# Attention of a two-layer hybrid DiT with the keys on the partitions: row maxima from a first pass, no transposes of the probabilities, row sums by additions

## The chip, the cores and the metric

One core of a Trainium2 chip runs the whole program. The time is the device time of one execution in microseconds (us). A core has five engines with a queue each that they work off in order: TensorE (PE, with its weight loads as PEld), VectorE (DVE), ScalarE (ACT), GpSimd (POOL) and SyncE (SP), which here only issues DMAs.

## The reference

Two layers over 256 context and 1024 latent tokens of width 1024. Each layer normalises and modulates its input, projects it once, gives the parts to three branches (gated DeltaNet, GDN; latent attention, MLA; gated linear attention, GLA), gates each and projects the sum of widths back. The change lies in the attention of the MLA branch: 8 heads, queries and keys of 64 + 32 (the 32 are rotated, and shared by all heads on the key side), values of 64; context queries read context keys, latent queries read all 1280.

```python
def attend(q, k, v):
    s = jnp.einsum('bqhd,bkhd->bhqk', q, k).astype(jnp.float32) * MLA_SCALE
    p = jax.nn.softmax(s, axis=-1).astype(v.dtype)
    return jnp.einsum('bhqk,bkhd->bqhd', p, v)
# out = attend(...) * silu(z); layer 1 needs no context output
```

Everything is f32, and results have to agree with f32.

## The kernel before

The tokens are ten tiles of 128 (i = 0, 1 context, 2 to 9 latent), the heads four pairs m with hh = 0 and 1. A layer runs the input projection, prepares GDN, projects q, k and v up (`up`) into arrays in memory (qn_d, qpe_d, kn_d, kpe_d, v_d), then runs `attend`, then the output projection (`proj_start`, `proj`). Beside `up` and `attend` runs a background generator: the GDN scan of 20 steps (tiles kS, Tr, F), the preparation of GLA, its 7 levels, and the GLA scan of 10 steps (`gla_scan`, L926 to L992: kdt transposes the keys, ktl is their copy, gO the output, oL its sum, gF the state's addition, Sl the state; head_norm writes the result to y_d). All of its matmul groups use one PSUM buffer (tag "l", one buffer). `run` takes one background step after each yield of `attend` (L1481); whatever is left comes after. The framework's scheduler then sorts each engine's instructions by its own estimate of the times, and the engines run the order that it fixes.

Scores need more than one pass of the fast f32 format (fp32r), so q and k are split in a rounded part (hi: kTh, qTh, made by ACT) and the remainder (lo: kTl, qTl, made by POOL). `mm3` (L253) adds three products:

```python
mm(out, lh, rh, start=first, stop=False)
mm(out, lh, rl, start=False, stop=False)
mm(out, ll, rh, start=False, stop=last)
```

`attend` goes over units: a pair m, a 128-query tile i and a head hh (a context unit takes both tiles at once): 72 in layer 0, 64 in layer 1. The queries of a unit are stationary (128x128), and the 1280 keys move, so scores have queries on the partitions: sa holds 1024 keys (two buffers of two banks), sb 256. `first` and `second` issue them; DVE reduces the maxima (L1206, L1225, L1226), ACT makes the exponentials with the maximum as bias and their sums as a by-product (L1228, L1227). `transposed` turns the probabilities on PE, 128x128 at a time into ptr (L1243), and ACT or DVE copies them out (PT, L1247). After four units `output` multiplies: 20 matmuls O (L1255) with 64 columns of vv stationary and 256 queries of PT moving, head 0 into partitions 0 to 63 and head 1 into 64 to 127; the sums reach the same layout through a diagonal matrix dg times ones (L1266, L1267). ztl (the gate) and the division end it. `load_k` fetches the keys of a pair through one stage buffer kTs (L1150, L1151), `load_q` the queries, both some units ahead.

Of the kernel before, what the change touches and what calls it, by code (L numbers as in the profile page):

```python
# [18 lines left out]
NT = 10  # L19
T = 1280  # L20
# [8 lines left out]
KB = 4  # L29
QB = 4  # L30
QSB = 2
PTB = 2
YMB = 1
PB = 3
ATB = 3
KVB = 3
LA = 3
# [6 lines left out]
class Net:  # L44
# [969 lines left out]
    def up(self, l):  # L1014
# [79 lines left out]
        for a, b in GROUPS:  # L1094
            ps = self.g("kpt", "u")
            w = 128 * (b - a)
            for i in range(a, b):
                nc.tensor.transpose(ps[0:32, 128 * (i - a):128 * (i - a) + 128], ko[:, i, :], self.ident)
            t = uo()
            A.copy(t[0:32, :w], ps[0:32, :w])  # L1100
            P.memset(t[32:64, :w], 0.0)
            nc.sync.dma_start(self.kpe_d[l][:, 128 * a:128 * b], t[0:64, :w])
# [31 lines left out]
    def attend(self, l, fill=None):  # L1134
        nc, sp = self.nc, self.ap
# [3 lines left out]
        lt0 = CT if last else 0  # L1139
        kTs, vv = {}, {}  # L1140

        def load_k(m):
            kTs[m] = []
            vv[m] = self.ab.tile([128, T], F32, name="vv", tag="vv", bufs=2)
            nc.sync.dma_start(vv[m].rearrange("p (i c) -> p i c", c=128),
                              self.v_d[l][:, :, 128 * m:128 * m + 128].rearrange("i p c -> p i c"))
            for hh in range(2):
                st = self.ab.tile([128, T], F32, name="kTs", tag="kTs", bufs=1)
                hi, lo = (self.ab.tile([128, T], F32R, name=nm, tag="kT", bufs=KB) for nm in ("kTh", "kTl"))
                nc.sync.dma_start(st[0:64], self.kn_d[l][m, 64 * hh:64 * hh + 64])  # L1150
                nc.sync.dma_start(st[64:128], self.kpe_d[l])  # L1151
                A.copy(hi, st)  # L1152
                P.tensor_tensor(lo, st, hi.bitcast(F32), ALU.subtract)
                kTs[m].append((hi, lo))

        qTs = {}

        def load_q(m, i0):
            t0 = 128 * i0
            st = sp.tile([128, 2, 256], F32, name="qTs", tag="qTs", bufs=QSB)  # L1160
            hi, lo = (sp.tile([128, 2, 256], F32R, name=nm, tag="qT", bufs=QB) for nm in ("qTh", "qTl"))
            nc.sync.dma_start(st[0:64], self.qn_d[l][m, :, t0:t0 + 256].rearrange("(h p) t -> p h t", h=2))
            for r in (64, 96):
                nc.sync.dma_start(st[r:r + 32], self.qpe_d[l][2 * m:2 * m + 2, :, t0:t0 + 256].rearrange("h p t -> p h t"))
            A.copy(hi, st)
            P.tensor_tensor(lo, st, hi.bitcast(F32), ALU.subtract)
            zt = sp.tile([128, 256], F32, name="ztl", tag="ztl", bufs=2)
            nc.sync.dma_start(zt, self.zt_d[l][m, :, t0:t0 + 256])
            qTs[m, i0] = (hi, lo, zt)

        groups = [(m, i) for m in range(4) for i in range(lt0, NT, 2)]
        units = [(m, i + j, hh) for m, i in groups for hh in range(2) for j in range(1 if i < CT else 2)]
        sb, mxs, sas, ps, PT, rds = {}, {}, {}, {}, {}, {}

        def scores(u, dst, c0, cn, j=0):
            m, i, hh = units[u]
            q, k = [t[:, hh] for t in qTs[m, i - i % 2][0:2]], kTs[m][hh]
            J = slice(128 * (i % 2 + j), 128 * (i % 2 + j) + 128)
            self.mm3(dst, q[0][:, J], q[1][:, J], k[0][:, c0:c0 + cn], k[1][:, c0:c0 + cn], True, True)

        def prepare(u):

            for v in (u, min(u + LA, len(units) - 1)):
                m, i, hh = units[v]
                if m not in kTs:
                    load_k(m)
                if (m, i - i % 2) not in qTs:
                    load_q(m, i - i % 2)

        def first(u, c0):  # L1190

            m, i, hh = units[u]
            if i < CT:
                if c0 == 0:
                    sas[u] = sa = self.ps.tile([128, 1024], F32, name="sa", tag="sa", bufs=2)[:, 0:512]
                    for j in range(2):
                        scores(u, sa[:, 256 * j:256 * j + 256], 0, 256, j)
                    mxs[u] = mx = sp.tile([128, 2], F32, name="mx", tag="mx", bufs=4)
                    V.tensor_reduce(mx, sa.rearrange("p (j k) -> p j k", j=2), AX.X, ALU.max, negate=True)
                return  # L1200
            if c0 == 0:
                sas[u] = self.ps.tile([128, 1024], F32, name="sa", tag="sa", bufs=2)
            scores(u, sas[u][:, c0:c0 + 512], c0, 512)
            if c0 == 512:
                mxs[u] = mx = sp.tile([128, 2], F32, name="mx", tag="mx", bufs=4)
                V.tensor_reduce(mx[:, 0:1], sas[u], AX.X, ALU.max, negate=True)  # L1206

        def second(u):

            m, i, hh = units[u]  # L1210
            mx, ta = mxs.pop(u), sas.pop(u)
            if hh == 0 and i % 2 == 0:
                rds[m, i] = sp.tile([128, 2, 2, 2], F32, name="rd", tag="rd", bufs=3)
            r = rds[m, i - i % 2][:, hh, i % 2, :]
            ps[u] = p = self.ab.tile([128, T], F32, name="P", tag="P", bufs=PB)
            if i < CT:
                for j in range(2):
                    J = slice(256 * j, 256 * j + 256)
                    A.activation(p[:, J], ta[:, J], AF.Exp, bias=mx[:, j:j + 1], accum_out=r[:, j:j + 1])
                return  # L1220
            if u // 2 not in sb:
                sb[u // 2] = self.ps.tile([128, 512], F32, name="sb", tag="sb", bufs=1)
            tb = sb[u // 2][:, 256 * (u % 2):256 * (u % 2) + 256]
            scores(u, tb, 1024, 256)
            V.tensor_reduce(mx[:, 1:2], tb, AX.X, ALU.max, negate=True)  # L1225
            V.tensor_tensor(mx[:, 0:1], mx[:, 0:1], mx[:, 1:2], ALU.min)  # L1226
            A.activation(p[:, 1024:T], tb, AF.Exp, bias=mx[:, 0:1], accum_out=r[:, 1:2])  # L1227
            A.activation(p[:, 0:1024], ta, AF.Exp, bias=mx[:, 0:1], accum_out=r[:, 0:1])  # L1228

        def transposed(u, ka):  # L1230
            m, i, hh = units[u]
            nk = NT if i >= CT else 4
            if ka >= nk:
                return
            if ka == 0 and i % 2 == 0:
                PT[hh] = self.ab.tile([128, NT, 256], F32, name="PT", tag="PT", bufs=PTB)
            p, kb = ps[u], min(ka + 4, nk)
            if kb == nk:
                ps.pop(u)
# [38 lines left out]
        for u in range(n + 1):  # L1278
            if u + 1 < n:
                prepare(u + 1)  # L1280
# [303 lines left out]
```

## Time and profile before

| | us |
|---|---|
| median of 3 runs (lowest to highest) | 2279.92 (2273.16 to 2285.7) |
| profiled execution: its time / span | 2280.18 / 2278.4 |
| PE busy | 2043.3 (90%) |
| DVE, ACT, POOL busy | 1291.6, 941.1, 743.7 |
| attention of layer 0 (632 to 1075): PE, DVE, ACT, POOL busy | 408.73, 312.73, 241.78, 168.78 of 443 |
| attention of layer 1 (1755 to 2171): PE, DVE, ACT, POOL busy | 382.50, 290.18, 220.17, 157.69 of 416 |

A row of the timeline gives the start, the busy time, the engine, the line, the operation, the written tile and the read ones, shapes and count of a group; in brackets stand the idle time ahead of it on that engine and what ended it. "x4" is four records, and an f32 matmul has two records, a matmul of hi and lo parts one. Ends on PE are modelled: the distance from start to start says what a matmul costs, and the busy time has a tail in it. PEclk is the clock that was granted, as a share of full speed.

### The profile page before, as it was taken

The numbers are of one execution on the slowest core, as the hardware profiler recorded it, in microseconds if no ns is written. First come the engines' busy times: TensorE is split into PE (matmuls) and PEld (weight loads), VectorE is DVE, ScalarE is ACT, GpSimd is POOL, SyncE is SP. The second block draws the span as 40 slices with busy tenths as digits, with TensorE's granted clock in tenths as the row PEclk, the third lists the DMA queues.
The fourth block names the chain that finished last, engine by engine and source line by source line (L and its number), as shares of the span: only waits on it lengthen the run. The fifth ranks groups of instructions, "written<-read, shape, count | busy, mean of one in ns | idle before, by whom it ended". The sixth has DMA issues, their size and how long they took to land.

```text
span 2278.4 us, 44490 instructions
## 1 busy us (share of the span) xinstructions
PE 2043.3 (90%) x17820; PEld 1709.8 (75%) x17820; DVE 1291.6 (57%) x2187; ACT 941.1 (41%) x1926; POOL 743.7 (33%) x936
## 2 busy tenths in 40 slices
PE   5998997999989988898897998976987999899998
PEld 3987896886767766676897987875876776667688
DVE  3446685323447689656425356795233677975634
ACT  3246311533235466555204356212542445564531
POOL 1233265122234543214103322381123264421410
PEclk8999998899989999999898999998998999899999
DMA  7111343258742231113424212424266242101352
GB/s 296 47 62 61 105 119 113 84 200 284 220 109 76 76 111 36 40 48 121 161 93 171 65 36 81 136 69 115 90 197 168 58 115 96 54 24 50 100 155 103
DMA packets 207551, 247.34 MB, mean 109 GB/s; under 512 B 60976, under 2 KB 164464, under 8 KB 203760
## 3 DMA queue, kind: packets, MB, share of 16 engines
q1 hardware_dynamic: 207344, 244.49, 34.1%
q8 instruction: 140, 2.29, 0.4%
q14 instruction: 67, 0.55, 0.1%
HBM read 168.14 MB, written 76.28 MB: 107 GB/s over the span
## 4 chain that ended last, share of the span: by engine, by line
PE 46%; DVE 13%; ACT 5%; DMA 5%; issue 3%; POOL 2%; SPq 1%; DVEq 0%; POOLq 0%; ACTq 0%
PE O L1255 6%; PE ptr L1243 4%; PE po L257 3%; PE po L255 3%; PE po L256 3%; PE sa L255 3%; PE sa L256 2%; PE sa L257 2%; PE ptk L255 1%; PE ptk L256 1%; PE ptk L257 1%; DVE XT L634 1%; DVE X L636 1%; PE kS L730 1%; DVE acc L345 1%
## 5 line engine op out<-in xcount | busy, mean ns | idle before, releaser
L255 PE MATMUL ptk<-whi,hhi 128*128 128x256 f32 (+1 forms) x912 | 263.6, 290 | 6.1 <-DVE ev L297 2.2
L257 PE MATMUL ptk<-whi,hlo 128*128 128x256 f32 (+1 forms) x912 | 261.9, 288 | 1.8 <-POOL hlo L238 1.7
L256 PE MATMUL ptk<-wlo,hhi 128*128 128x256 f32 (+1 forms) x912 | 261.7, 287 | 0.4 <-DVE wlo L250 0.4
L1243 PE MATMUL ptr<-c_id,P 128*128 128x128 f32 x1312 | 203.6, 283 | 27.8 <-ACT PT L1247 18.8
L1243 PEld LDWEIGHTS ptr<-c_id,P 128*128 128x128 f32 x1312 | 151.2, 143 | 78.1 <-ACT PT L1247 29.9
L1247 ACT COPY PT<-ptr 128x512 f32<-128x512 f32 (+1 forms) x256 | 122.3, 480 | 211.1 <-PE ptr L1243 209.7
L256 PE MATMUL pin<-hlo,whi 128*128 128x512 f32 (+1 forms) x544 | 201.6, 371 | 1.6 <-issue 1.6
L255 PE MATMUL pin<-hhi,whi 128*128 128x512 f32 (+1 forms) x544 | 202.5, 372 | 0.0
L257 PE MATMUL pin<-hhi,wlo 128*128 128x512 f32 (+1 forms) x544 | 201.8, 372 | 0.0
L255 PEld LDWEIGHTS ptk<-whi,hhi 128*128 128x128 f32 x912 | 179.4, 197 | 10.8 <-issue 4.3
L1206 DVE TENSOR_REDUCE mx<-sa 128x1 f32<-128x1024 f32 x128 | 156.2, 1220 | 53.6 <-PE sa L257 53.0
L257 PEld LDWEIGHTS ptk<-whi,hlo 128*128 128x128 f32 x912 | 178.8, 197 | 5.3 <-POOL hlo L238 3.0
L256 PEld LDWEIGHTS ptk<-wlo,hhi 128*128 128x128 f32 x912 | 179.4, 197 | 3.1 <-issue 2.0
L1255 PE MATMUL O<-PT,vv 128*64 128x256 f32 x1312 | 169.6, 388 | 1.7 <-ACT PT L1247 0.9
L255 PE MATMUL po<-wohi,yh 128*128 128x256 f32 x576 | 164.4, 286 | 4.4 <-DVE yl L1353 2.1
L256 PE MATMUL po<-wolo,yh 128*128 128x256 f32 x576 | 164.0, 285 | 0.0
L257 PE MATMUL po<-wohi,yl 128*128 128x256 f32 x576 | 162.6, 285 | 0.0
L1228 ACT ACTIVATE P<-sa,mx 128x1024 f32<-128x1024 f32 x128 | 142.2, 1111 | 0.0
L1255 PEld LDWEIGHTS O<-PT,vv 128*64 128x64 f32 x1312 | 97.2, 138 | 59.0 <-issue 11.9
L255 PE MATMUL sa<-kTh,qTh 128*128 128x512 f32 (+1 forms) x272 | 118.3, 436 | 21.1 <-ACT kTh L1152 15.2
L250 POOL TENSOR_TENSOR wlo<-wst,whi 128x1024 fp32r<-128x1024 f32 x32 | 84.1, 2639 | 127.5 <-ACT whi L249 126.4
L256 PEld LDWEIGHTS pin<-hlo,whi 128*128 128x128 f32 x544 | 105.6, 194 | 19.7 <-issue 4.4
(341 smaller groups left out, 5030.6 us busy)
## 6 DMA issues: line engine op xcount, KB each, us to landing
wada<-in_w_ada_dram SPq DMA_DIRECT2D x24, 1024.0 KB
wst<-in_w_in_dram SPq DMA_DIRECT2D x48, 512.0 KB
kv<-ktv_d SPq DMA_DIRECT2D x80, 128.0 KB
wost<-in_w_out_dram SPq DMA_DIRECT2D x16, 512.0 KB
xt<-in_x_all_dram SPq DMA_DIRECT2D x10, 512.0 KB
at_d<-D SPq DMA_DIRECT2D x4, 1280.0 KB
kn_d<-uo SPq DMA_DIRECT2D x20, 256.0 KB
v_d<-uo SPq DMA_DIRECT2D x20, 256.0 KB
```

Source lines behind the costliest of these rows:

```text
L250: E.tensor_tensor(lo[:, h], st, hi[:, h].bitcast(F32), ALU.subtract)
L255: mm(out, lh, rh, start=first, stop=False)
L256: mm(out, lh, rl, start=False, stop=False)
L257: mm(out, ll, rh, start=False, stop=last)
L345: nc.vector.scalar_tensor_tensor(a, raw[:, tap:tap + 1282], cw[:, ti, tap:tap + 1], a, ALU.mult, ALU.add)
L634: E.tensor_tensor(tmp, Xv[B, G, 0:k, k].unsqueeze(3).broadcast_to([q, n, nr, ncl]), Xv[B, G, k, k + 1:32].unsqueeze(2).broadcast_to([q, n, ...
L636: E.tensor_tensor(dst, dst, tmp, ALU.add)
L1206: V.tensor_reduce(mx[:, 0:1], sas[u], AX.X, ALU.max, negate=True)
L1228: A.activation(p[:, 0:1024], ta, AF.Exp, bias=mx[:, 0:1], accum_out=r[:, 0:1])
L1243: nc.tensor.transpose(tp[:, 128 * (k - ka):128 * (k - ka) + 128], p[:, 128 * c:128 * c + 128], self.ident)
L1247: (V.tensor_copy if ka == 4 else A.copy)(PT[hh][:, ka:kb, 128 * (i % 2):128 * (i % 2) + 128], tp[:, 0:128 * (kb - ka)].rearrange("p (k t) ...
L1255: mm(po[64 * h2:64 * h2 + 64, 0:256], vv[m][:, 128 * k + 64 * h2:128 * k + 64 * h2 + 64], PT[h2][:, k, :], start=(k == 0), stop=(k == nk - 1))
```

## The change

A unit is now a pair m and a group of queries: 256 context queries, or 512 latent ones (two groups), both heads: 12 units in layer 0, 8 in layer 1. `maxima` runs one unit ahead: a score product of the hi parts alone over the 96 rows of q and k, with queries on the partitions, into S (three banks, one buffer); DVE reduces all 1280 at once; small matmuls r turn each column of negative maxima into a row, and ACT writes that into row 96 of qTh. Row 96 of the keys is 1, so the product of hi parts subtracts the maximum by itself. `exponentials` then takes 128 keys as stationary and 512 queries moving, into s (two buffers), and ACT's Exp writes pT (six buffers) without bias. pT has the keys on the partitions, so `output` can use it as it is: per key tile and head one matmul of 64 columns of vv, into O. The row sums come from additions of the pT tiles into acc, 13 of 18 in a latent unit on POOL and 5 on DVE, and one matmul with ones per head at the end (`finish`). kTl is made by DVE when a unit first needs it, from a second fetch of the keys through the same single stage buffer; kTh keeps four buffers. The generator yields 357 times in layer 0 and 321 in layer 1, where it yielded 452 and 400.

```diff
@@ kernel constants (KB, QB, QSB, PTB, YMB, PB, LA) @@
...
@@ in up(), where the rotated part of the keys is written @@
             A.copy(t[0:32, :w], ps[0:32, :w])
             P.memset(t[32:64, :w], 0.0)
+            P.memset(t[32:33, :w], 1.0)
@@ attend(), whose old body (L1134 to L1293) all goes @@
...
+        kh, kl, vv, qs, mxs, po, acc, pts = {}, {}, {}, {}, {}, {}, {}, {}
+        units = ([] if last else [(m, 0) for m in range(4)]) + [(m, g) for m in range(4) for g in (1, 2)]
+        def toks(u):
+            return ((0, 256), (256, 512), (768, 512))[units[u][1]]
+        def keys(u):
+            m, g = units[u]
+            return (m, g > 0), (T if g else 256)
+        def stage(m, hh, n):
+            st = self.ab.tile([128, T], F32, name="kTs", tag="kTs", bufs=1)
+            nc.sync.dma_start(st[0:64, 0:n], self.kn_d[l][m, 64 * hh:64 * hh + 64, 0:n])
+            nc.sync.dma_start(st[64:128, 0:n], self.kpe_d[l][:, 0:n])
+            return st[:, 0:n]
+        def load_kh(u):
+            c, n = keys(u)
+            kh[c] = []
+            for hh in range(2):
+                hi = self.ab.tile([128, T], F32R, name="kTh", tag="kTh", bufs=4)[:, 0:n]
+                A.copy(hi, stage(c[0], hh, n))
+                kh[c].append(hi)
+            vv[c] = self.ab.tile([128, T], F32, name="vv", tag="vv", bufs=2)[:, 0:n]
+            nc.sync.dma_start(vv[c].rearrange("p (i c) -> p i c", c=128),
+                              self.v_d[l][0:n // 128, :, 128 * c[0]:128 * c[0] + 128].rearrange("i p c -> p i c"))
+        def load_kl(u):
+            c, n = keys(u)
+            kl[c] = []
+            for hh in range(2):
+                lo = self.ab.tile([128, T], F32R, name="kTl", tag="kTl", bufs=2)[:, 0:n]
+                V.tensor_tensor(lo, stage(c[0], hh, n), kh[c][hh].bitcast(F32), ALU.subtract)
+                kl[c].append(lo)
+        def load_q(u):
+            m = units[u][0]
+            t0, w = toks(u)
+            st = sp.tile([128, 2, 512], F32, name="qTs", tag="qTs", bufs=1)[:, :, 0:w]
+            hi, lo = (sp.tile([128, 2, 512], F32R, name=nm, tag="qT", bufs=4)[:, :, 0:w] for nm in ("qTh", "qTl"))
+            nc.sync.dma_start(st[0:64], self.qn_d[l][m, :, t0:t0 + w].rearrange("(h p) t -> p h t", h=2))
+            nc.sync.dma_start(st[64:96], self.qpe_d[l][2 * m:2 * m + 2, :, t0:t0 + w].rearrange("h p t -> p h t"))
+            P.memset(st[96:128], 0.0)
+            A.copy(hi, st)
+            P.tensor_tensor(lo, st, hi.bitcast(F32), ALU.subtract)
+            qs[u] = (hi, lo)
+            mxs[u] = sp.tile([128, 8], F32, name="mx", tag="mx", bufs=2)
+        def maxima(u):
+            c, n = keys(u)
+            t0, w = toks(u)
+            if c not in kh:
+                load_kh(u)
+            load_q(u)
+            q, mx = qs[u][0], mxs[u]
+            def scores(dst, hh, j, c0, cn):
+                mm(dst, q[0:96, hh, 128 * j:128 * j + 128], kh[c][hh][0:96, c0:c0 + cn], start=True, stop=True)
+            if n < T:
+                S = self.S()
+                for hh in range(2):
+                    for j in range(2):
+                        scores(S[:, 512 * hh + 256 * j:512 * hh + 256 * j + 256], hh, j, 0, 256)
+                V.tensor_reduce(mx[:, 0:4], S[:, 0:1024].rearrange("p (x k) -> p x k", k=256), AX.X, ALU.max, negate=True)
+                yield
+            for hh in range(2):
+                for j in range(w // 128 if n == T else 0):
+                    S = self.S()
+                    for c0, cn in CHUNKS:
+                        scores(S[:, c0:c0 + cn], hh, j, c0, cn)
+                    V.tensor_reduce(mx[:, 4 * hh + j:4 * hh + j + 1], S[:, 0:T], AX.X, ALU.max, negate=True)
+                    yield
+                r = self.g("r", "r")
+                for j in range(w // 128):
+                    x = w // 128 * hh + j
+                    mm(r[96:97, 128 * j:128 * j + 128], mx[:, x:x + 1], self.ident, start=True, stop=True)
+                A.copy(q[96:97, hh, :], r[96:97, 0:w])
+                yield
+        def exponentials(u, k, hh):
+            c, n = keys(u)
+            w = toks(u)[1]
+            if c not in kl:
+                load_kl(u)
+            s = self.g("s", "s")
+            J = slice(128 * k, 128 * k + 128)
+            self.mm3(s[:, 0:w], kh[c][hh][:, J], kl[c][hh][:, J], qs[u][0][:, hh], qs[u][1][:, hh], True, True)
+            p = self.ab.tile([128, 512], F32, name="pT", tag="pT", bufs=6)
+            A.activation(p[:, 0:w], s[:, 0:w], AF.Exp)
+            pts[u, k, hh] = p
+        def output(u, k):
+            c, n = keys(u)
+            w, nk = toks(u)[1], n // 128
+            if k == 0:
+                po[u] = self.g("O", "o")
+            for hh in range(2):
+                mm(po[u][64 * hh:64 * hh + 64, 0:w], vv[c][:, 128 * k + 64 * hh:128 * k + 64 * hh + 64],
+                   pts[u, k, hh][:, 0:w], start=(k == 0), stop=(k == nk - 1))
+            for hh in range(2):
+                if k == 0:
+                    continue
+                if k == 1:
+                    acc[u, hh] = self.ab.tile([128, 512], F32, name="acc", tag="acc", bufs=3)
+                a = acc[u, hh][:, 0:w]
+                (V if hh and k % 2 else P).tensor_tensor(a, pts[u, 0, hh][:, 0:w] if k == 1 else a, pts[u, k, hh][:, 0:w], ALU.add)
+            if k == nk - 1:
+                finish(u)
+        def finish(u):
+            m = units[u][0]
+            t0, w = toks(u)
+            zt = sp.tile([128, 512], F32, name="ztl", tag="ztl", bufs=1)[:, 0:w]
+            nc.sync.dma_start(zt, self.zt_d[l][m, :, t0:t0 + w])
+            o = sp.tile([128, 512], F32, name="osb", tag="osb", bufs=1)[:, 0:w]
+            A.copy(o, po[u][:, 0:w])
+            r = self.g("sum", "r")
+            for hh in range(2):
+                mm(r[64 * hh:64 * hh + 64, 0:w], self.ones[:, 0:64], acc[u, hh][:, 0:w], start=True, stop=True)
+            rc = sp.tile([128, 512], F32, name="rc", tag="rc", bufs=1)[:, 0:w]
+            V.reciprocal(rc, r[:, 0:w])
+            P.tensor_tensor(zt, zt, rc, ALU.mult)
+            V.scalar_tensor_tensor(o, o, 0.5, zt, ALU.mult, ALU.mult)
+            nc.sync.dma_start(self.yT_d[l][m, :, t0:t0 + w], o)
+        ahead = maxima(0)
+        for _ in ahead:
+            yield
+        before = None
+        for u in range(len(units)):
+            nk = keys(u)[1] // 128
+            todo = 0
+            if u + 1 < len(units):
+                ahead, todo = maxima(u + 1), (10 if keys(u + 1)[1] == T else 3)
+            for k in range(nk):
+                for hh in range(2):
+                    exponentials(u, k, hh)
+                    yield
+                if before:
+                    output(*before)
+                before = (u, k)
+                yield
+                for _ in range(-(-todo // (nk - k))):
+                    todo -= 1
+                    next(ahead, None)
+                    yield
+            for _ in ahead:
+                pass
+        output(*before)
+        yield
@@ in run() @@
-                self.ps, self.psb = self.pool(st, "psB", space=PSUM), {"t": 2}
+                self.ps, self.psb = self.pool(st, "psB", space=PSUM), {"S": 1, "s": 2, "o": 1, "r": 1}
```

On PE the output of one unit in layer 1 reads so before (sa and sb are scores, gF a state of the GLA scan):

```order
L255 MATMUL sb<-kTh,qTh 128x256
L256 MATMUL sb<-kTl,qTh 128x256
L257 MATMUL sb<-kTh,qTl 128x256
L1255 MATMUL O<-PT,vv 64x256 x15
L980 MATMUL gF<-gvt,ktl 128x256 x2
L1255 MATMUL O<-PT,vv 64x256 x5
L1267 MATMUL O<-dg,ones 64x256 x2
L1243 MATMUL ptr<-c_id,P 128x128 x4
L255 MATMUL sa<-kTh,qTh 128x512
```

And in the last unit after (s is one key tile's scores of one head, the matmuls O are of one head and the other in turn):

```order
L248 MATMUL s<-qTh,kTh 128x512
L249 MATMUL s<-qTl,kTh 128x512
L250 MATMUL s<-qTh,kTl 128x512
L1236 MATMUL O<-pT,vv 64x512
L248 MATMUL s<-qTh,kTh 128x512
L249 MATMUL s<-qTl,kTh 128x512
L250 MATMUL s<-qTh,kTl 128x512
L1236 MATMUL O<-pT,vv 64x512
```

The matmuls of the two heads stood next to each other, 20 at a stretch; now three products of the scores stand between one and the next.

Where the GLA scan falls on PE at the end of layer 1, before:

```order
L255 MATMUL sa<-kTh,qTh 128x512
L256 MATMUL sa<-kTl,qTh 128x512
L961 MATMUL gO<-Sl,QQ 128x256
L964 MATMUL gO<-gvt,A_19168 128x64 x4
L961 MATMUL gO<-Sl,QQ 128x256
L1243 MATMUL ptr<-c_id,P 128x128 x6
L257 MATMUL sa<-kTh,qTl 128x512
L1243 MATMUL ptr<-c_id,P 128x128 x4
L255 MATMUL sb<-kTh,qTh 128x256
```

And after, from the last matmuls of attention (gsc belongs to GLA's levels, sum is the last step of the last unit) into the scan:

```order
L1236 MATMUL O<-pT,vv 64x512
L886 MATMUL gsc<-qx_18102,kc 64x256 x4
L1236 MATMUL O<-pT,vv 64x512 x2
L1257 MATMUL sum<-acc,ones 64x512 x2
L943 MATMUL kdt<-c_id,KK 128x128 x2
L973 MATMUL gF<-gvt,ktl 128x256 x2
L943 MATMUL kdt<-c_id,KK 128x128 x2
L973 MATMUL gF<-gvt,ktl 128x256 x2
L943 MATMUL kdt<-c_id,KK 128x128 x2
```

The steps of the scan stood between the scores and transposes of attention; now all nine that change the state stand behind its last matmul. In layer 0 three of the nine stand before the last matmul of attention and six behind.

## Rows read from the trace of the kernel before

**Rows 1.** The page: its span, and the busy time of PE.
```profile
span 2278.4 us, 44490 instructions
PE 2043.3 (90%) x17820; PEld 1709.8 (75%) x17820; DVE 1291.6 (57%) x2187; ACT 941.1 (41%) x1926; POOL 743.7 (33%) x936
```

**Rows 2.** Two stretches of layer 1: length; PE, PEld, DVE, ACT, POOL busy; PEclk; DMA.
```profile
1755.00:2171.00 416.00, 382.50 (x3472) 291.97 (x3473) 290.18 (x547) 220.17 (x502) 157.69 (x190) 0.95 0.26 76
1900.00:2050.00 150.00, 129.47 (x1199) 97.82 (x1199) 126.42 (x219) 92.70 (x206) 62.86 (x77) 0.91 0.20 62
```

**Rows 3.** Timeline of PE, steady attention beside the GDN scan.
```profile
1804.61 1.15 PE L730 MATMUL kS<-Sg,KQ 64*64 64x64 f32 x32
...
1806.03 0.39 PE L256 MATMUL sa<-kTl,qTh 128*128 128x512 f32 x1
1806.26 0.39 PE L257 MATMUL sa<-kTh,qTl 128*128 128x512 f32 x1
...
1807.19 0.82 PE L1243 MATMUL ptr<-c_id,P 128*128 128x128 f32 x6
1807.94 0.68 PE L740 MATMUL Tr<-r,TT 64*64 64x64 f32 x16
...
1828.64 1.15 PE L730 MATMUL kS<-Sg,KQ 64*64 64x64 f32 x32
```

**Rows 4.** Timeline of PE, an output, then a gate matmul of full width.
```profile
2149.24 4.54 PE L1255 MATMUL O<-PT,vv 128*64 128x256 f32 x40
2153.61 0.60 PE L1267 MATMUL O<-dg,ones 128*64 128x256 f32 x4
2154.14 0.66 PE L1243 MATMUL ptr<-c_id,P 128*128 128x128 f32 x4
...
2154.99 1.02 PE L1331 MATMUL gate<-dgc,ones 128*128 128x512 f32 x2
```

**Rows 5.** Timeline of all engines, steps of the GLA scan in layer 1.
```profile
2117.78 1.03 PE L980 MATMUL gF<-gvt,ktl 128*128 128x256 f32 x4
...
2118.84 0.69 DVE L982 TENSOR_TENSOR Sl<-gF,c_bdm 128x512 f32<-128x512 f32 x1 [0.17 <-PE gF L980]
...
2121.06 0.38 PE L950 MATMUL kdt<-c_id,KK 128*128 128x128 f32 x2
...
2122.28 0.36 ACT L952 COPY ktl<-kdt 128x256 f32<-128x256 f32 x1
...
2122.69 0.70 PE L961 MATMUL gO<-Sl,QQ 128*128 128x256 f32 x2 [0.35 <-ACT ktl L952]
...
2124.07 0.65 PE L961 MATMUL gO<-Sl,QQ 128*128 128x256 f32 x2
...
2124.75 0.76 DVE L975 TENSOR_TENSOR oL<-gO,oL 128x256 f32<-128x256 f32 x2 [0.28 <-PE gO L961]
```

**Rows 6.** Busy us by engine, layer 0, attention's end to the output projection.
```profile
1075.88:1090.43 14.55, 5.56 (x25) 4.13 (x24) 2.89 (x6) 7.26 (x14) 9.14 (x6) 0.66 0.85 287
```

**Rows 7.** Groups of instructions: xcount | busy us, mean ns | idle before.
```profile
L1206 DVE TENSOR_REDUCE mx<-sa 128x1 f32<-128x1024 f32 x128 | 156.2, 1220 | 53.6 <-PE sa L257 53.0
L1228 ACT ACTIVATE P<-sa,mx 128x1024 f32<-128x1024 f32 x128 | 142.2, 1111 | 0.0
L1247 DVE COPY PT<-ptr 128x512 f32<-128x512 f32 x128 | 87.5, 683 | 18.7 <-PE ptr L1243 18.0
L1166 POOL TENSOR_TENSOR qTl<-qTs,qTh 128x512 fp32r<-128x512 f32 x36 | 48.2, 1340 | 145.8 <-ACT qTh L1165 138.3 <-PE ptr L1243 7.4
```

**Rows 8.** Chain of waits at layer 0's first keys: start, us, what.
```profile
624.61 6.75 DMA kTs<-kpe_d
```

**Rows 9.** Timeline of DVE and POOL while keys are loaded, layer 0.
```profile
817.35 4.26 DVE L906 TENSOR_TENSOR KK<-KK,al 128x640 f32<-128x640 f32 x2
...
817.66 3.27 POOL L1153 TENSOR_TENSOR kTl<-kTs,kTh 128x1280 fp32r<-128x1280 f32 x1 [2.36 <-ACT kTh L1152]
...
821.60 0.81 DVE L906 TENSOR_TENSOR QQ<-QQ,al 128x640 f32<-128x640 f32 x1
```

More of the change, by code (lines that the diff above doesn't have):

```diff
@@ L28 @@
 UPS = 28
[L29 to L34, printed above, removed]
 ATB = 3
 KVB = 3
-LA = 3
 CV = 5
@@ L1138, in attend @@
         V, A, P = nc.vector, nc.scalar, nc.gpsimd
[L1139 to L1146, printed above, removed]
-            for hh in range(2):
[L1148 to L1164, printed above, removed]
+        kh, kl, vv, qs, mxs, po, acc, pts = {}, {}, {}, {}, {}, {}, {}, {}
@@ L1165, in load_q @@
             A.copy(hi, st)
             P.tensor_tensor(lo, st, hi.bitcast(F32), ALU.subtract)
[L1167 to L1195, printed above, removed]
-                    for j in range(2):
[L1197 to L1239, printed above, removed]
-            tp = self.g("ptr", "t")
-            for k in range(ka, kb):
-                c = k if i >= CT else 2 * (k % 2) + k // 2
-                nc.tensor.transpose(tp[:, 128 * (k - ka):128 * (k - ka) + 128], p[:, 128 * c:128 * c + 128], self.ident)
-            if i < CT:
-                A.copy(PT[hh][:, 0:2, :], tp.rearrange("p (k t) -> p k t", t=256))
-            else:
-                (V.tensor_copy if ka == 4 else A.copy)(PT[hh][:, ka:kb, 128 * (i % 2):128 * (i % 2) + 128],
-                                                       tp[:, 0:128 * (kb - ka)].rearrange("p (k t) -> p k t", t=128))
@@ L1274, in attend @@
-        n = len(units)
-        prepare(0)
-        first(0, 0)
-        first(0, 512)
-        for u in range(n + 1):
-            if u + 1 < n:
-                prepare(u + 1)
-            if u < n:
-                second(u)
+            qs[u] = (hi, lo)
[12 more added lines that the diff above has]
+                for hh in range(2):
+                    for j in range(2):
+                        scores(S[:, 512 * hh + 256 * j:512 * hh + 256 * j + 256], hh, j, 0, 256)
[14 more added lines that the diff above has]
+                yield
@@ L1283, in attend @@
                 yield
-            for x in range(3):
-                if u > 0:
-                    transposed(u - 1, 4 * x)
+                for _ in range(-(-todo // (nk - k))):
+                    todo -= 1
+                    next(ahead, None)
                     yield
-                if u + 1 < n and x < 2:
-                    first(u + 1, 512 * x)
-                    yield
-            if u > 0 and (u == n or units[u][0:2] not in (units[u - 1][0:2], (units[u - 1][0], units[u - 1][1] + 1 - 2 * (units[u - 1][1] % 2)))):
-                output(units[u - 1][0], units[u - 1][1] - units[u - 1][1] % 2)
-                yield
+            for _ in ahead:
+                pass
```

22 lines of the change are left out of this document (removed).

## The prediction

> **What bounds the kernel now.** First the page's head: TensorE (PE) is busy for 2043 us of a 2278.4 us span [rows 1]. Then the same table over the stretches that the change rewrites: attention of layer 1 lasts 416 us with PE busy for 382 and VectorE (DVE), ScalarE (ACT) and GpSimd (POOL) for 290, 220 and 158 [rows 2]; layer 0 is alike. At full clock PE is the bound there, and only in the middle, where GLA runs beside attention, does it idle for some 20 us (150 us, 129 busy). So the question is what one unit of attention costs on PE, and which work of the other engines stops being hidden.
>
> The steady state gives that price. Between the two kS groups at 1804.61 and 1828.64 us lie four old units (128 queries of one head each) and two GDN steps [rows 3]. A GDN step is a kS group of 1.15 us and three groups like Tr of 0.68, less the tails that the next matmul covers, some 2.9 together. So a unit takes (24.03 - 5.9)/4 = 4.54 us, and the 8 old units that hold the work of one new unit (512 queries, both heads) take 36.3. Starts alone give less: a 512-column product of the scores starts every 0.233 us, so scores are 3 x (2 x 0.233 + 0.117) = 1.75, ten transposes at 0.105 (from the x6 row) 1.05, and the output 1.2: 4.0. The other 0.54 us is spread over some 6 changes of the kind of matmul, 0.09 each.
>
> **PE, per new unit.** Scores: 20 key tiles x head, three products of 0.233 each: 14.0. Transposes: gone. First pass: 8 products over 1280 keys, hi parts only, 0.585 each: 4.7. Rows of maxima: 8 small matmuls of a full 128 columns in f32, about 0.21 each (twice the transpose's 0.105): 1.7. Sums: 1.1.
>
> The output is the term that decides. Before, 40 matmul records of 256 columns and 4 of dg for one output went into 4.90 us, 0.109 each from start to start, since two heads write to two halves of the partitions and run side by side; full-width gF and gate records take 0.213 per 256 columns (4 of gF in 1.03 us, a tail of 0.17 in it: dg's 0.60 less 4 x 0.109) and 0.43 per 512 (2 of gate in 1.02) [rows 4, 5]. In the order after, three score products stand between the matmul of the one head and that of the other, almost everywhere: nothing runs beside either. So 20 matmuls of two 512-column records cost 0.853 each, 17.1 us, where side by side they would cost 8.5.
>
> Sum of starts: 14.0 + 17.1 + 4.7 + 1.7 + 1.1 = 38.6. Changes of kind: about 56 (in and out of each of 20 outputs, plus 8 S passes and few others) x 0.085 = 4.8, so 43.4; I take 43. The unknown is the change from a 64-wide to a full-width matmul: the nearest row has O to ptr at 0.09 (dg from 2153.61, 4 x 0.109, ptr at 2154.14) [rows 4]; the lower end is nothing (38.6), the upper end the whole tail of a record, 0.166, on 40 of the changes (45.2). The Trainium skill, "TensorEngine Tiling (Array Packing)", Key Properties, says that a change of tiling mode drains TensorE; taken as the whole tail that would be 45.2 in place of 43. The row here shows about half of it.
>
> So +6.7 a unit, x 8 units = **+54 per layer**; in layer 0 the four context units add 1.2 each, +5.
>
> **What leaves PE's cover.** In the order before, the GLA scan's nine steps stand among the last attention units of layer 1, and PE is the bound there. In the order after all nine stand behind the last sum. So PE's own part leaves the stretch (two short steps of 1.3, seven of 0.2 + 2.0 + 1.0: -25), and the scan then runs alone. One step alone, from its pieces [rows 5]: kdt 0.38, ktl's copy 0.36, gO from 2122.69 to 2124.72 2.03, two additions 0.76, gF 1.03, Sl 0.69, together 5.25, all in a chain because the "l" buffer in PSUM is one and each group waits for the reader of the last; with six hand-overs of some 0.1 (the additions' row shows 0.28, Sl's 0.17) 5.9. Nothing is left beside it but head_norm, which is shorter. Two short steps of 2.9, seven of 5.9 and the end: **+50**. In layer 0 about six full steps come last: -16 and **+36**.
>
> The turn to the output projection: in layer 0 the wait for y and gate, 14.55 us with PE busy for 5.6, loses its 9 us of idle to the scan's own time [rows 6]: -9. In layer 1 the last scan step's y goes through memory before the turn: +5 for that.
>
> **Start and key changes.** Layer 1 begins with a first pass of 8 products with nothing beside it: product 0.585, reduce about 1.5 (1.22 for 1024 [rows 7], by length 1.53 for 1280), 0.3 for the hand-overs, and a single S buffer, so 2.4 x 8 = 19.2 where PE needs 4.7 (counted): **+13**, with row hand-overs. In layer 0 the short context unit comes first: 0. At each change of keys the third product waits for kTl: the second head's key stage is issued only when the first's subtraction freed the one buffer, and its DMA landed 6.75 us after issue [rows 8]. PE has about 9 us of other products ahead of that, the subtract waits for the old unit's last use: 2 to 4 us each, **+12** in layer 0, **+9** in layer 1. Relief: DVE loses the PT copy (0.68 per old unit [rows 7]) and sb's reduce, and gains 0.3 (1280 keys for 1024) and 5 additions per new unit of some 0.69 (Sl's), 0.4 per old one; and more PE time per unit covers GLA's pauses: I give back 12 of the 20 us per layer.
>
> **Sum.** Layer 1: 54 - 25 + 50 + 13 + 9 - 12 + 5 = +94. Layer 0: 54 + 5 - 16 + 36 + 0 + 12 - 12 - 9 = +70. Together +164; the profiled execution took 2280.18 (its span and 1.8 around it), the median 2279.92, which is the same. 2280 + 164 is 2444, **2440** in round numbers.
>
> **What I cost at nothing.** ACT: 20 Exp of 128x512, each under the 1.11 us of 128x1024 [rows 7], so under 22 us in a unit of 43; PE is the cover. POOL: 13 additions, the query remainder and zt, 16 instructions like the 128x512 subtraction of 1.34 and the memsets, 21 of 43. Key loads rise from 32 to 96 issues on SP, in front of them stand only transfers that have a unit's time. The small matmuls r wait for DVE's reduce, and the unit's next score products are queued behind them on PE; in the order they stand some products behind the S pass, which covers 1.5 us of reduce. y's DMA, the gate's load and the division of one unit lie beside the next.
>
> **Rivals.**
> (B) The two heads still run side by side. The products between them would have to cost only a change (0.1): -8.5 x 16 = -136 on the sum, **2304**. For it: records of the two halves do run side by side where they are adjacent [rows 4]. Against: a score product uses all columns, and nothing in the trace runs beside one.
> (C) The vector side binds. While POOL subtracted kTl, two DVE multiplications of 128x640 took 4.26 us, where the next of that shape took 0.81 [rows 9]: two engines that hold one another. If POOL's 16 instructions per unit go from 1.34 to 2.7 so, they take 43, and GLA's own POOL work, some 8 us per 43 (of the 62.9 in 150 that are not attention's [rows 2]), becomes 16: 59 in a unit of 43, 16 over in the about 9 units beside GLA: +145, **2585**. pT's six buffers then fill and PE stops. Against it: at PE's pace POOL has 22 us of slack per unit, and most of DVE's work reads PSUM. The Trainium skill, "SBUF — State Buffer", Who interferes with whom, has an exclusive lock, for a whole instruction, between a DVE operation with two SBUF inputs and a POOL one that reads SBUF; the trace agrees (4.26 us).
> (D) The other side: the halves run side by side and changes cost nothing, 30.1 a unit in place of 43: -13 x 16 = -208 on the sum, **2232**, faster. Its place is the O matmul between score products, its price then 0.43 each, and it decides where O and its two changes take under 0.56 us: the other terms (+164 less 6.7 x 16, so +57, 3.6 per unit) need a unit below 36.3 - 3.6 = 32.7, and 32.7 - 21.5 (scores, first pass, rows, sums) over 20 is 0.56. The trace has 0.43 side by side and 0.85 alone; for it speaks only that adjacent halves do overlap; against, the order itself.
> (E) What the scan and start add is hidden after all while PE is as before: within 0.5%.
>
> **How the numbers follow.** About 0.5% (11 us) is what can be told from no change. Chances: halves alone and scan last, 2440: 0.70, with its own range 2340 to 2540 (a unit of 38.6 to 45.2: -70 to +35; scan and turn between 0 and +80 where the sum has +41; key changes 0 to +40 where it has +21; not all at one end). B 0.08, C 0.11, D 0.06, E 0.05. D gives faster with a little of E: 0.07; same 0.05; the rest slower: 0.88. The range takes in B and the lower part of C and leaves out D: 2300 to 2560.
>
> **What would show it.** After: O records of 128x512 with 0.43 between starts, s at 0.233, 0.08 to 0.1 between kinds; PE's span per unit 43; S reduce near 1.5; after the last sum of layer 1 some 50 us in which PE is busy for a half or less; the kTs DMA ahead of L250 in the chain of waits at each change of m; POOL busy for under 60% of attention. Wrong would be: O pairs at 0.43 in all (B, D), additions of 2.5 us and PE idle waiting for pT or s (C), the scan's steps lying among score products in time.

## The result and the profile after

The changed kernel takes 2579.55 us (median of 4, 2573.54 to 2582.84) where the one before takes 2281.74: a ratio of 1.131 (95% interval 1.127 to 1.135), 298 us more. The forecast was 2440, in a range of 2300 to 2560: the direction was right, the size was not, and the time lies outside the range.

Where the time went is seen by cutting both profiled executions at the same three places in each layer: the last matmul of the query projection (qp), attention's last matmul, and the first matmul of the output projection (po). The rows of the windows give the length and then the busy time of PE, PEld, DVE, ACT and POOL, the granted clock, the DMA share and GB/s. Before, attention of layer 0, its turn to po, and attention of layer 1 (whose turn is 0.4 us):

```profile
617.20:1074.90 457.70, 415.44 (x3787) 307.83 (x3785) 317.78 (x610) 243.63 (x569) 174.66 (x221) 0.96 0.26 76
1074.90:1090.40 15.50, 6.51 (x27) 4.53 (x27) 3.73 (x8) 7.23 (x14) 9.14 (x6) 0.68 0.84 282
1742.70:2170.80 428.10, 387.45 (x3586) 296.12 (x3585) 294.79 (x557) 221.41 (x504) 163.80 (x197) 0.94 0.27 79
```

After, attention and what follows it up to po, for layer 0 and then layer 1:

```profile
618.00:1155.40 537.40, 492.38 (x2912) 232.62 (x2910) 322.28 (x368) 185.36 (x334) 269.65 (x243) 0.93 0.25 67
1155.40:1248.20 92.80, 50.19 (x150) 31.82 (x149) 39.41 (x65) 21.86 (x40) 28.27 (x20) 0.57 0.40 129
1892.20:2365.40 473.20, 442.07 (x2659) 202.70 (x2657) 278.36 (x311) 157.15 (x264) 251.24 (x220) 0.95 0.24 64
2365.40:2469.90 104.50, 58.44 (x159) 37.01 (x159) 29.42 (x56) 18.56 (x36) 27.02 (x18) 0.53 0.29 96
```

Attention is longer by 80 and 45 us, and PE's busy time in it by 77 and 55; what stands behind it, by 77 and 104, at 0.57 and 0.53 of the clock. The rest of the program is 4 us shorter. More than half of the loss is therefore not in attention, but behind it.

**One key tile on PE.** The steady state of layer 1, in the place of [rows 3, 4]:

```profile
1975.32 0.50 PE L248 MATMUL s<-qTh,kTh 128*128 128x512 f32 x1
1975.66 0.39 PE L249 MATMUL s<-qTl,kTh 128*128 128x512 f32 x1
1975.89 0.40 PE L250 MATMUL s<-qTh,kTl 128*128 128x512 f32 x1
1976.21 1.07 PE L1236 MATMUL O<-pT,vv 128*64 128x512 f32 x2
1977.22 0.50 PE L248 MATMUL s<-qTh,kTh 128*128 128x512 f32 x1
...
1979.11 0.85 PE L1195 MATMUL S<-kTh,qTh 96*128 96x512 f32 x3
1979.89 0.38 PE L1214 MATMUL r<-c_id,mx 128*1 128x128 f32 x2
1980.20 0.68 PE L752 MATMUL F<-vn,at 64*64 64x64 f32 x16
```

From one first score product to the next it takes 1.90 us: three products (0.70), an O matmul of two records that nothing runs beside (0.853), and 0.35 for the changes: O starts 0.09 late, the product behind it starts 1.00 and not 0.853 after it, and the second product 0.34 after the first where it is 0.23 elsewhere. So a change costs at three places; the forecast had 0.17 for the way in and out together. A first pass product takes 0.78 with its changes (0.585 without), a row r 0.31. A unit is then 20 x 1.90 + 8 x 0.78 + 8 x 0.31 + 2 = 48.7 us, where 43 was forecast. That is the price where every key tile reads like this one; in 16 of the 168 pairs of the whole trace the two heads' matmuls stand next to each other all the same.

**The tail.** A step of the GLA scan behind attention in layer 1, from kdt to the next kdt, beside [rows 5]:

```profile
2381.40 0.69 PE L943 MATMUL kdt<-c_id,KK 128*128 128x128 f32 x2 [0.78 <-DVE Sl L975]
2382.61 1.22 PE L954 MATMUL gO<-Sl,QQ 128*128 128x256 f32 x2 [0.52 <-ACT ktl L945]
2383.62 1.80 PE L957 MATMUL gO<-gvt,A 128*128 128x64 f32 x8
2385.22 1.17 PE L954 MATMUL gO<-Sl,QQ 128*128 128x256 f32 x2
2387.12 2.08 PE L973 MATMUL gF<-gvt,ktl 128*128 128x256 f32 x4 [0.74 <-ACT oL L966]
2389.98 0.69 PE L943 MATMUL kdt<-c_id,KK 128*128 128x128 f32 x2 [0.79 <-DVE Sl L975]
```

The step takes 8.58 us and not 5.9: gF, 1.03 us in [rows 5], takes 2.08. The profile grants 0.53 of the clock in this stretch, and at this step the lower of the two levels (0.50 from 2374 to 2437). PE had stood at 1.00 from 2300 until attention ended and for 5 us more; the chain then leaves PE idle between almost every two groups.

**The background falls behind from the start.** A GDN step after, on PE and DVE (the r of DVE is what Tr reads, vn what the next F reads; the r of PE is a row of maxima):

```profile
1963.27 1.15 PE L723 MATMUL kS<-Sg,KQ 64*64 64x64 f32 x32
...
1965.14 0.42 DVE L726 TENSOR_TENSOR r<-kv,r 128x256 f32<-128x256 f32 x1
...
1968.14 0.38 PE L1214 MATMUL r<-c_id,mx 128*1 128x128 f32 x2
1968.44 0.85 PE L1195 MATMUL S<-kTh,qTh 96*128 96x512 f32 x3
1969.22 0.68 PE L733 MATMUL Tr<-r,TT 64*64 64x64 f32 x16
...
1970.74 0.41 DVE L735 TENSOR_TENSOR vn<-Tr,bes 128x256 f32<-128x256 f32 x1
...
1974.71 0.68 PE L741 MATMUL F<-vn,kv 64*64 64x64 f32 x16
...
1985.68 1.15 PE L723 MATMUL kS<-Sg,KQ 64*64 64x64 f32 x32
```

DVE's r is there at 1965.56, and Tr starts at 1969.22, since the rest of one key tile's 1.90, a whole one, a row of maxima and a first pass product stand ahead of it in PE's queue. A step takes 22.4 us from kS to kS, 12.0 on average before (two steps in 24.03 [rows 3]). The last kS of layer 1 comes 264 us after qp (158 before), and the scan begins 474 us after it (301), with attention just over.

### The profile page after: what moved, and what is told of

The parts are those of the page before. It is cut to its first block, busy times and chain, and to the rows that moved or that the text cites. A ratio compares the mean times of both kernels' runs of the same rounds, so it can differ in the third digit from the quotient of the medians.

```text
span 2580.8 us, 40939 instructions
## 1 busy us (share of the span) xinstructions
PE 2278.8 (88%) x16300; PEld 1607.4 (62%) x16300; DVE 1335.0 (52%) x1807; ACT 844.8 (33%) x1506; POOL 971.4 (38%) x1018
## 4 chain that ended last, share of the span: by engine, by line
PE 52%; DVE 9%; DMA 7%; issue 3%; ACT 3%; POOL 2%; SPq 1%; DVEq 0%; POOLq 0%; ACTq 0%
PE O L1236 11%; PE s L248 5%; DMA kTs<-kpe_d 4%; PE S L1195 3%; PE s L250 3%; PE po L248 3%; PE s L249 3%; PE po L249 3%; PE po L250 3%; PE ptk L249 1%; PE ptk L248 1%; DMA wost<-in_w_out_dram 1%; PE ptk L250 1%; PE r L1214 1%; DVE XT L627 1%
## 5 line engine op out<-in xcount | busy, mean ns | idle before, releaser
L1236 PE MATMUL O<-pT,vv 128*64 128x512 f32 (+1 forms) x672 | 345.6, 617 | 3.1 <-ACT osb L1254 2.1
L1244 POOL TENSOR_TENSOR acc<-acc,pT 128x512 f32<-128x512 f32 x192 | 258.5, 1352 | 192.5 <-ACT pT L1227 164.4
L1227 ACT ACTIVATE pT<-s 128x512 f32<-128x512 f32 (+1 forms) x336 | 194.9, 586 | 397.1 <-PE s L250 364.4
L1209 DVE TENSOR_REDUCE mx<-S 128x1 f32<-128x1280 f32 x128 | 190.2, 1486 | 162.6 <-PE S L1195 162.3
L248 PE MATMUL s<-qTh,kTh 128*128 128x512 f32 (+1 forms) x336 | 164.9, 491 | 14.5 <-ACT qTh L1215 11.1
L248 PEld LDWEIGHTS s<-qTh,kTh 128*128 128x128 f32 x336 | 64.0, 190 | 160.8 <-ACT pT L1227 96.3
L1195 PE MATMUL S<-kTh,qTh 96*128 96x512 f32 (+1 forms) x400 | 120.5, 411 | 35.3 <-DVE mx L1209 19.7
L1195 PEld LDWEIGHTS S<-kTh,qTh 96*128 96x128 f32 x400 | 69.7, 202 | 116.8 <-issue 50.7
L250 PE MATMUL s<-qTh,kTl 128*128 128x512 f32 (+1 forms) x336 | 134.8, 402 | 6.6 <-DVE kTl L1169 6.6
L1236 PEld LDWEIGHTS O<-pT,vv 128*64 128x64 f32 x672 | 62.6, 137 | 116.7 <-issue 108.7
```

What stands on the lines that cost most here:

```text
L1195: mm(dst, q[0:96, hh, 128 * j:128 * j + 128], kh[c][hh][0:96, c0:c0 + cn], start=True, stop=True)
L1209: V.tensor_reduce(mx[:, 4 * hh + j:4 * hh + j + 1], S[:, 0:T], AX.X, ALU.max, negate=True)
L1227: A.activation(p[:, 0:w], s[:, 0:w], AF.Exp)
L1236: mm(po[u][64 * hh:64 * hh + 64, 0:w], vv[c][:, 128 * k + 64 * hh:128 * k + 64 * hh + 64], pts[u, k, hh][:, 0:w], start=(k == 0), stop=(k ...
L1244: (V if hh and k % 2 else P).tensor_tensor(a, pts[u, 0, hh][:, 0:w] if k == 1 else a, pts[u, k, hh][:, 0:w], ALU.add)
```

## The experiments

For each kernel the four lengths of the table are those of the windows above: from qp to attention's last matmul, and from there to po.

| kernel | us (median) | attention 0 | behind it | attention 1 | behind it |
|---|---|---|---|---|---|
| before | 2280 | 457.7 | 15.5 | 428.1 | 0.4 |
| the change | 2579.6 | 537.4 | 92.8 | 473.2 | 104.5 |
| e1 pairs | 2464.3 | 463.8 | 115.0 | 415.4 | 92.6 |
| e2 held order | 2504.4 | 593.5 | 18.7 | 515.1 | 4.0 |
| e3 key fetches | 2569.0 | 515.9 | 106.0 | 466.7 | 104.4 |
| e4 no additions | 2558.3 | 516.5 | 93.5 | 472.5 | 96.6 |
| e5 e1 + e2 + e3 | 2411.6 | 527.0 | 23.6 | 473.4 | 6.9 |
| e6 the same, with a lag | 2407.5 | 539.0 | 9.9 | 478.0 | 2.3 |
| e7 matmuls in the scan's waits | 2556.5 (one run) | 528.1 | 96.5 | 474.1 | 81.7 |
| e8 e6 without additions | 2345.3 | 501.4 | 8.0 | 465.8 | 0.0 |
| e9 first pass twice | 2604.7 | 568.1 | 77.6 | 492.8 | 87.7 |

**e1: the two heads' output matmuls side by side.** In outline:

```diff
 # in output(), with last_s the last score matmul traced, last_o the last of a pair
+o = the PE instructions of both heads' mm
+self.behind(o[0], last_s[-1])           # order on PE alone, no wait
+each of o behind the one before it; scores traced later stand behind o[-1]
```

> The output matmuls of the two heads of a key tile are put next to each other on PE by order edges alone (the first behind the second head's scores, the next scores behind the second); nothing else changes. Theory 1 (halves alone cost twice): per key tile 6 score products, one change each way and two halves side by side, about 2.6 us where the changed kernel's trace has 3.8, so 12 us per unit of 512 queries, 16 units: -190 on 2580, less what the GLA chain then leaves idle; 2390 to 2450. Theory 2 (the vector side binds): unchanged, 2570 to 2590. Theory 3 (halves never overlap here, only changes cost): 0.35 us per key tile, -50: 2530.

Measured: 2464.33, a ratio to before of 1.080 (1.077 to 1.083), 115 us under the change. On PE:

```profile
2008.99 0.50 PE L257 MATMUL s<-qTh,kTh 128*128 128x512 f32 x1
...
2010.27 0.39 PE L259 MATMUL s<-qTh,kTl 128*128 128x512 f32 x1
2010.59 1.08 PE L1252 MATMUL O<-pT,vv 128*64 128x512 f32 x4
2011.60 0.73 PE L1205 MATMUL S<-kTh,qTh 96*128 96x512 f32 x2
```

Both heads' four records take 1.01 us, as long as one head's two did alone; a key tile takes 2.61 instead of 3.80, as theory 1 has it. The time lies above theory 1's 2390 to 2450, since less comes of it than 96 us a layer: PE's busy time in attention falls by 81 and 70 us (in layer 1 from 442 to 372.5), its idle time grows by 7 and 12 (in layer 1 to 43), so attention gains 74 and 58, and the tail stays. That layer 1's attention is now shorter than before is no gain: most of the scan (41 us of PE time in both layers together, as priced) is not in it.

**e2: the scan held among attention's matmuls.** In outline:

```diff
-for _ in self.attend(l):
-    if bg is not None and next(bg, bg) is bg:
-        bg = None
+after every 4th yield of attend: one background step; its last PE instruction is `last`
+each PE instruction that attend traces from then on: self.behind(it, last)
```

> One background step per four yields of attention, and PE's attention matmuls after such a step may not stand ahead of its PE matmuls, so the GLA scan stands among attention's matmuls; work unchanged. Theory 1 (the scan and the turn behind attention cost 105 us in layer 1 and 92 in layer 0, where before had 0 and 15): most of this goes, less the scan's own PE time (41 us): 2430 to 2490. Rival (the tail is only moved: the chain of the background ends where it ended, and attention now waits for it): above 2550. In the scan's rows gF x4 should take 1.1 us beside attention, where it took 2.1 alone at half clock.

Measured: 2504.36 (1.098, 1.095 to 1.101), 75 under the change, less than theory 1 said and more than its rival. The tail goes as forecast (18.7 and 4.0 us behind attention instead of 92.8 and 104.5, and gF takes 1.03 to 1.13 us), but attention grows by 56 and 42. In the windows of attention in layers 0 and 1, and of GLA's levels in layer 1, PE waits:

```profile
612.80:1206.30 593.50, 482.56 (x3038) 251.64 (x3037) 350.91 (x422) 198.06 (x360) 287.31 (x257) 0.88 0.25 71
1871.20:2386.30 515.10, 424.29 (x2819) 227.33 (x2815) 317.66 (x365) 171.37 (x294) 270.39 (x234) 0.91 0.27 72
2050.00:2200.00 150.00, 102.47 (x883) 56.88 (x880) 115.49 (x136) 62.55 (x113) 85.78 (x76) 0.86 0.21 63
```

PE is idle for 111 and 91 us there (45 and 31 in the change). Its busy time falls by 10 and 18 us although the scan is now in it, since e2 is not the pure change of place that it was meant to be: its edges also moved attention's own matmuls, and in 92 of the 168 pairs the two heads' output matmuls now stand next to each other (16 in the change, 164 to 167 where e1's edit is in). Part of e1's gain is therefore already in e2.

**e3: faster key fetches.** A stage buffer of its own for the second head's context keys; a layer's first keys take kTh and kTl from one fetch.

> The second head's context keys get a stage buffer of their own, and the first key set of each layer takes kTh and kTl from one fetch. Theory 1 (the stage buffer's chain of fetches costs some 25 us more than priced at layer 0's start and 25 at layer 1's): -20 to -40, 2540 to 2560. Rival (PE waits there for something else, the maxima): 2570 to 2585.

Measured: 2568.96 (1.126, 1.123 to 1.129): 11 us less, between the two, and with intervals that overlap (the change has 1.127 to 1.135). Layer 0's attention is shorter by 21.5 us, but 13 come back behind it; layer 1's is shorter by 6.5. The fetches are a chain as forecast (rows of the chain of waits of the change at layer 1's start):

```profile
1897.07 7.16 DMA kTs<-kpe_d
1906.11 8.36 DMA kTs<-kpe_d
1916.34 4.79 DMA kTs<-kpe_d
1924.73 3.74 DMA kTs<-kpe_d
```

Taking one or two links out is worth some 10 us at most, so they are not the main cause.

**e4: 16 of 18 additions of a unit left out.**

> Leaves out 16 of the 18 additions of the row sums in each latent unit (POOL's 13 among them), so the sums are not the reference's. Rival C (the vector side binds, POOL's additions hold pT): -100 to -150, 2430 to 2480. Theory 1 (PE and the tail bind): within 1%, 2555 to 2585.

Measured: 2558.25 (1.122, 1.118 to 1.125): 21 us, at the edge of what theory 1 allowed and far from rival C. In the change the additions' mean on POOL is 1.35 us, as priced:

```profile
L1244 POOL TENSOR_TENSOR acc<-acc,pT 128x512 f32<-128x512 f32 x192 | 258.5, 1352 | 192.5 <-ACT pT L1227 164.4
```

So the time forecast for C came out nearly (2585 for 2580), but its mechanism did not.

**e5 and e6: the three edits together**, without and with a lag (a background step per three yields, attention up to six steps ahead).

> The three edits together: pairs of output matmuls, one background step per four yields with attention's matmuls held behind it, and the faster key fetches. Theory 1: the tail's 115 and 93 us of the paired kernel go, the scan's 41 us of PE time come back into attention, and where GLA's chain is late PE waits for it (the held order alone had PE busy for 102 of 150 us there): 2300 to 2350. Rival (the gains of pairs and held order are the same time twice): 2420 or more.

> As the one before with one background step per three yields, and attention allowed six background steps ahead of the one it is held behind, so that a late chain of GLA does not stop PE at once. Theory 1: 20 to 50 us less than the one before: 2270 to 2320, next to the kernel before. Rival (the background's own chain sets the end of attention, not its place in PE's queue): the same as the one before.

Measured: 2411.57 (1.059, 1.055 to 1.063) and 2407.50 (1.058, 1.054 to 1.061). Both misses: the gains do not add up, in part because e2 already held some of e1's, and the lag changes nothing, which is the time of e6's rival. PE in the attention of both layers of e6 (the second window reaches to po), in the 150 us beside GLA in layer 1, and the longest of its waits there:

```profile
616.60:1155.60 539.00, 440.09 (x3042) 253.67 (x3041) 361.42 (x426) 200.91 (x368) 294.25 (x262) 0.88 0.29 80
1823.40:2303.70 480.30, 399.71 (x2841) 231.62 (x2840) 330.06 (x372) 176.38 (x302) 276.45 (x236) 0.89 0.29 80
1990.00:2140.00 150.00, 105.49 (x837) 60.36 (x835) 110.63 (x137) 59.70 (x110) 82.69 (x74) 0.83 0.18 53
PE gsc L876 <- DMA KK<-gqk_d: 17.2, 1, 17.2
```

PE's busy time is within 25 and 12 us of before (415 and 387), the scan included; its idle time is 99 and 81, where before had 42 and 41. What is lost now is mostly time in which PE waits for the background: 47 and 41 us of the idle time stand ahead of the matmuls of GLA's levels (gsc), 3 and 4 before. The mechanism of e6's rival is not shown by this: the last scan step starts 100 and 91 us ahead of attention's end (36 and 50 before), so the background's chain does not set that end. Attention's matmuls were held while PE stood idle, and are worked off when the background is done. A looser hold, of the scan alone for instance, was not run.

**e7: two extra matmuls in each wait of the scan**, results unused.

> The GLA scan is traced behind attention (in layer 1 it stood there anyway; in layer 0 three steps more), and two extra matmuls (384 columns f32, result unused) stand in each of its three waits, so that PE is busy in them. Theory 1 (the step took 8.6 us for 5.9 since PE's clock was granted at half there, and rows of gF and gO took twice their time): layer 1's steps from kdt to kdt fall to 6 to 6.8 us, gF x4 to 1.0 to 1.2, PEclk near 1. Rival (the step is long because of hand-overs): 8.6 or more, as the extra matmuls only add.

Measured, a step with an output in layer 1 (L1500 is one of the extra matmuls):

```profile
2370.20 0.44 PE L952 MATMUL kdt<-c_id,KK 128*128 128x128 f32 x2
2370.48 0.60 PE L1500 MATMUL warm<-c_bdm,c_id 128*128 128x256 f32 x2
...
2373.92 1.13 PE L982 MATMUL gF<-gvt,ktl 128*128 128x256 f32 x4
...
2375.84 0.44 PE L952 MATMUL kdt<-c_id,KK 128*128 128x128 f32 x2
```

5.64 us a step, below the 6 to 6.8 of theory 1, with more work on PE than the 8.58 had; gF at 1.13. In windows, first the change's whole scan in layer 1, then this kernel's:

```profile
2365.40:2437.70 72.30, 52.01 (x148) 34.82 (x149) 22.88 (x39) 7.57 (x20) 7.01 (x5) 0.54 0.21 66
```

```profile
2363.20:2413.20 50.00, 44.62 (x249) 38.22 (x248) 22.00 (x39) 7.76 (x20) 6.83 (x5) 1.00 0.28 90
```

The clock is at its upper level throughout, and the scan takes the 50 us that the prediction had. The clock alone cost 22 us there. In layer 0 nothing shows in the total (96.5 us behind attention for 92.8), as three more steps stand behind it. e7 is one run, but the trace of e9 (below) has the same chain without extra matmuls at both levels. While the granted clock is still 1.00 (2405.0 to 2422.0) a step takes 5.73 us:

```profile
2410.66 0.44 PE L943 MATMUL kdt<-c_id,KK 128*128 128x128 f32 x2 [0.78 <-DVE Sl L975]
2416.39 0.44 PE L943 MATMUL kdt<-c_id,KK 128*128 128x128 f32 x2 [0.78 <-DVE Sl L975]
```

At 0.50 (2430.3 to 2447.9) the step from 2430.35 to 2439.17 takes 8.82.

**e8: e6 without the additions.**

> The three edits with the lag, and 16 of the 18 additions of a latent unit left out (the sums are not the reference's). In the kernel with the edits PE is idle for 80 us of layer 1's attention, 45 of them in the 150 us beside GLA. Theory A (POOL's additions stand in the queue ahead of GLA's and GDN's POOL work and slow its chain): -30 to -50, 2360 to 2380. Theory B (GLA's chain is as long as it is, and was hidden before only because its place in PE's queue was free): -5 to -15, 2393 to 2403.

Measured: 2345.27 (1.030, 1.027 to 1.032), 62 under e6. That is on theory A's side and beyond its range; theory B is out. The same edit that gave 21 us while PE was the bound gives 62 when PE waits for the background. The run does not say by which way: POOL's queue (theory A), two engines that hold one another (rival C), or pT's buffers were not tried apart. Beside GLA in layer 1 PE's busy time rises only from 105 to 110 of 150 us. Attention as a whole gains 38 us in layer 0 and 12 in layer 1; in layer 0 the first scan step comes 317 us after qp where e6 had 339, so 22 of the 38 lie ahead of the scan.

**e9: each product of the first pass twice.**

> The changed kernel with each product of the first pass over 1280 keys done twice into the same place. PE binds attention: 3 products, 0.585 us, 8 in each of 16 units: +75; 2640 to 2660 (a little less where the longer attention takes some of the scan under it). Rival (the first pass lies in time that PE has free): under +25, below 2605.

Measured: 2604.74 (1.143, 1.139 to 1.147), +25, by the total just at the rival's bound. The windows say more: PE's busy time in attention grows by 40 and 32 (71 in both, 75 priced), attention by 31 and 20, since PE's idle time takes a third of it, and the longer attention takes 15 and 17 of the scan back under it. PE binds attention, with some slack.

## Why the prediction failed, step by step

The sum lacks 138 us (302 by the profiles, 164 forecast). They split by its own terms as follows; the rest of the program, -4, belongs to none:

- **O alone costs twice: right.** e1 shows it: 3.80 against 2.61 us a key tile. Rivals B and D, which needed the halves to overlap across the scores, are out.
- **Changes of kind at 0.085: wrong.** 0.35 us per O and 0.2 per S in the rows. By PE's busy time, with the scan's share put back as priced, a layer needs 80 and 93 us more where 54 and 59 were forecast: 26 and 34 of the 138. I had priced the way in and out of O from one row [rows 4], at 0.17 for both; the 0.10 between the first and the second product behind O I had not. The Trainium skill, "TensorEngine Tiling (Array Packing)", Key Properties, states that a change of tiling mode drains TensorE; the trace agrees in that each such change costs time (0.35 us per O). My estimate with a whole tail for each change, 45.2, was nearer to 48.7 than the 43 that I took, and still too low.
- **Start, key changes and relief: near.** Idle time in attention is 31 and 45 us after, 41 and 42 before; the forecast had +10 in layer 1 and 0 in layer 0, so -20 and +3 of the 138. One step of the sum was wrong in itself: 19.2 less 4.7 is 14.5 and not 13 for layer 1's first pass, without the row hand-overs.
- **The scan alone at 5.9 a step: wrong by the clock.** Its chain was right, to 0.3 us (e7), but PE's clock fell to its lower level in it: 8.58, shown by e7 and by the two levels in e9. +22 in layer 1, +21 in layer 0 (57 for 36).
- **The turn at +5 and -9: wrong.** 32 us lie between the scan's end and po in layer 1 (27 more than forecast) and 36 in layer 0 (29 more). The chain of waits of layer 1 shows what came from under attention:

```profile
2441.41 1.65 POOL ors L185
...
2449.57 6.40 DMA wost<-in_w_out_dram
...
2461.05 2.35 POOL wolo L243
2463.42 4.30 DMA wost<-in_w_out_dram
...
2467.79 1.04 ACT wohi L242
```

  The last head_norm on POOL, then the fetch of the output weights and their split, one behind another. Before, such rows lay beside attention's last units: the first two fetches of layer 1 started at 2150.5 and 2159.3, and attention ended at 2170.8. This term is read from the chain of waits; no run took it apart.
- **Rival C: out as forecast** (e4: 21 us, not 145). Its time was near 2580 by chance. That the additions do cost something shows in e8, when PE waits for the background; whether by C's mechanism is open.

The step that failed most is thus "What leaves PE's cover", with the turn in it: 99 of the 138 us (43 for the scan, 56 for the turn). The second is the price of the changes, 60. I found that the scan would stand alone, and priced it by rows taken from a PE that was busy. What else stood under the same cover, and at what clock PE would run without it, I did not ask.

What is not settled: how much of e6's loss comes of holding attention's matmuls behind the background. Up to the scan, the background in e6 is on its old timetable: GDN ends 171 and 168 us after qp (154 and 158 before), and the first scan step comes 339 and 302 us after it (337 and 301 before). Nor is it settled in which way the additions of e8 cost time; no run here took the two-input operations of DVE apart from them.

No version tried beats the kernel before. The nearest that computes the whole, e6, is 5.8% slower: in attention PE is idle for 57 and 40 us more than before and busy for 25 and 12 more, at a granted clock of 0.88 and 0.89 where before had 0.96 and 0.94. PE had nothing to give in return, since the first pass and its rows (8.7 us a unit by the rows above) put back on it what the transposes took (8 x 1.05 = 8.4 by the prediction's starts).

## What to carry to other kernels

When an order on one engine changes, list what was done beside it, and price that again without its cover: with the chain's hand-overs, at the clock that an engine with gaps is granted, and with all that waits behind it. A narrow matmul that shared the array with its twin cost double here when other work was put between the two; keep such pairs next to each other by an order edge. Read the price of a change of matmul shape from three starts, into, out of, and the one after.

## Not expected of the hardware

Two O records of one head take 1.00 us to the next start, four records of both heads 1.01: the second head is free when it stands next to the first. And more work made a chain faster: with two unused matmuls of together some 0.65 us in each wait, a scan step went from 8.58 to 5.64 us, as PE's granted clock stayed at 1.00 over the scan instead of 0.54.
